# Down projections of two FFNs as seven half products per pair of blocks, with more low parts summed by transfer

## The chip, the cores and the metric

The kernel runs on one core of a Trainium2 chip. The metric is the time of one execution on the device in microseconds. A profile is one execution taken by the hardware profiler; its times are microseconds unless marked ns. Engines are named as in the profile: PE (TensorE matmul), PEld (its weight loads), ACT (ScalarE), DVE (VectorE), POOL (GpSimd), SP (SyncE). POOL and SP issue the DMA transfers here; the accumulating ones go through POOL, plain loads mostly through SP.

## The reference

One encoder layer over 512 tokens with a model width of 1024, in float32. What concerns this change are the two FFNs; between them stands a mixer of a Fourier part and an attention part.

```python
def rms_norm(x, g):
    xf = x.astype(jnp.float32)
    y = xf * lax.rsqrt(jnp.mean(xf * xf, axis=-1, keepdims=True) + EPS)
    return (y * g.astype(jnp.float32)).astype(x.dtype)

def swiglu(h, w_gate, w_up, w_down):
    return (jax.nn.silu(h @ w_gate) * (h @ w_up)) @ w_down

x = x + 0.5 * swiglu(rms_norm(x, ffn1_norm), ffn1_w_gate, ffn1_w_up, ffn1_w_down)
...
x = x + 0.5 * swiglu(rms_norm(x, ffn2_norm), ffn2_w_gate, ffn2_w_up, ffn2_w_down)
return rms_norm(x, final_norm)
```

The hidden width D_FF is 2752, that is 21 columns of 128 and a tail of 64.

## The kernel before

**Numbers in two parts.** Matmuls run on the type float32r, which keeps fewer bits. So each operand is split: a high part is the value rounded by a cast on ScalarE (`nc.scalar.copy`, shown as CAST), and a low part is what is left, value minus high part. A product is three matmuls: high x high, high x low, low x high. The low part is made in one of two ways. `lows` (L130 for all callers) is one subtraction on VectorE. `rest_by_dma` (L159, L160) has ScalarE write the negated high part and POOL issue an accumulating transfer that adds the value to it from memory; what needs the low part then waits for the landing.

**Layout.** The tokens lie along the free dimension (S = 512) and the model width in eight blocks of 128 (KD = 8): `x[0]` to `x[7]`. All weights in two parts live in `ring`, twelve slots of 1024 elements (NS = 12), which `take` and `give` hand out first in, first out: a slot that comes free is written next by whoever takes it, so a cast into it waits for the last matmul that reads what was there.

**One FFN** (`ffn`) goes through the 21 columns in groups (`GROUPS1`, `GROUPS2`). The first group is computed plainly (`gate`, `evacuate`). From then on `seven` computes a column's gate and up products by the Strassen-Winograd scheme: seven products a11, a12, s1, s2, s4, s3, a22 of half the width in place of eight (`multiply`, lines L432, L436, L441). s1 to s4 are sums of weights that VectorE forms (`combine`, L406) in the temporaries `s12` and `s34`, of which there is one buffer each. `prepare` makes a column's weights while the column before is multiplied. The only low part that goes by transfer there is that of a22 (`single`, L400, 256 KB). The product a22 of a column stands behind a12 of the next one; that of the last column is called `rest` and stands inside the group's down projection. `seven` runs one column ahead of its group, so its last column belongs to the next group.

**Down projection.** For each of the eight blocks d, `down` loads the group's weights (`raw_dn`), makes the high part on ScalarE (L172) and the low part on VectorE (L130), and multiplies with the group's activations `at`, three 512-wide matmuls for each column (L186, out `dn`). `residual` (L575) then adds half of the sum to `x[d]`. With six columns in a group the columns 3 to 20 of the first FFN take three groups; the second FFN has groups of 6, 6 and 7.

**Order.** On PE and SP the order is that of the code. On ACT, DVE and POOL a scheduler has fixed the order when the kernel was built; at run time each engine works strictly in that order, so an instruction that waits holds up all behind it on its engine.

Of the kernel before, what the change touches and what calls it, by code (L numbers as in the profile page):

```python
# [88 lines left out]
def encoder(ctx, tc, A, out):  # L89
# [19 lines left out]
    def bank(name):  # L109
        return pp.tile([P, S], F32, tag="bank", name=name)  # L110
# [173 lines left out]
    def ffn(norm, after, wgu, wd, wdt, groups, opening, closing):  # L284
# [6 lines left out]
        with tc.tile_pool(name=f"act{n_}", bufs=1) as ap, tc.tile_pool(name=f"sums{n_}", bufs=2) as sp:  # L291
            room(ap, 128)
            acts = ap.tile([P, PLACES * 2 * S + ROOM], F32R, name=f"at{n_}")
            at = acts[:, FRONT + LOWER : FRONT + LOWER + PLACES * 2 * S].rearrange("p (n a b) -> p n a b", a=2, b=S)
            rt = ap.tile([P, 7 * KH * S + -(-PART_AT[-1] // ROOM) * ROOM], F32R, name=f"rt{n_}")
            wt, raws = [], {}
# [76 lines left out]
            def give(*ts):  # L373
                for t in ts:
                    taken[:] = [q for q in taken if q is not t]
                    (shared if any(t is q for q in slots[KD:]) else own).append(t)

            def prepare(j):

# [9 lines left out]
                def both(names, src):  # L389
                    hi, lo = (take() for _ in range(2))  # L390
                    nc.scalar.copy(hi, src)  # L391
# [27 lines left out]
            def seven(js, done):  # L419
# [37 lines left out]
                def step(j, w, n):  # L457
# [33 lines left out]
                    elif n == 9:  # L491
                        multiply(b["r"], "a22", "t4", w, False)
                        u, i = b["u"], place(j)
                        h, l = at[:, i, 0], at[:, i, 1]
                        kept(u[:, HALF:], b["r"], "a22" in WIDE)
                        nc.vector.tensor_tensor(out=u, in0=b["g"], in1=u, op=ALU.mult)
                        nc.scalar.copy(h, u)
                        lows(l, u, h)
                        del banks[j]
# [16 lines left out]
            def down(d, group, gi):  # L516
# [23 lines left out]

                return steps

            def token_weights(d, group):
# [36 lines left out]
            for gi, group in enumerate(groups):  # L580
# [4 lines left out]
                else:  # L585
# [19 lines left out]
                    def rest():  # L605
                        evacuate(at[:, place(n_plain - 1)], n_, pss[n_plain - 1], norm)

                def added(d, ps):
# [3 lines left out]
                    if ahead:  # L612
                        f, *a = ahead.pop(0)
                        f(*a)

                waiting, downs = [], []
                for d in range(KD):
# [35 lines left out]

    def evacuate(at, n_, pss, norm):
        g = tp.tile([P, S], F32, tag="g", name=f"g{n_}p")
        u = tp.tile([P, S], F32, tag="u", name=f"u{n_}p")
        h, l = at[:, 0], at[:, 1]
        if len(pss) == 2:
            nc.vector.tensor_tensor(out=g, in0=pss[0], in1=norm.rb, op=ALU.mult)
            nc.vector.tensor_tensor(out=u, in0=pss[1], in1=norm.rb, op=ALU.mult)  # L660
            nc.scalar.activation(g, g, AF.Silu)
            nc.vector.tensor_tensor(out=u, in0=g, in1=u, op=ALU.mult)
            nc.scalar.copy(h, u)
# [904 lines left out]
```

## Time and profile before

| | |
|---|---|
| times of three runs | 818.92, 818.92, 819.8 us (median 818.92) |
| the profiled execution's own time | 818.9 us |
| its span, first to last instruction | 817.1 us |
| mean granted clock | 0.998 |
| matmuls of the FFN columns (L432, L436, L441) | 2520 |
| matmuls of the down projections of whole blocks (L186, out `dn`) | 945 |
| accumulating transfers from POOL (L160) | 53 |

How to read the profile: a group of instructions is named by line, engine, operation and tiles (out<-in); "busy" is the time in which at least one of them ran, "mean ns" the length of one, "idle before" the time in which the engine stood still just before them and what ended it. A row of the timeline gives the start, the length, the engine, the line and how many instructions followed each other without a gap. Matmuls are pipelined, so the distance between starts says more than the length of one.

### The profile page before, as it was taken

What the parts mean: (1) busy time and instruction counts of PE and PEld (TensorE: products, weight loads), DVE (VectorE), ACT (ScalarE), POOL (GpSimd) and SP (SyncE); (2) the same over time, 40 slices, a digit from 0 to 9 for tenths busy, and PEclk for the clock granted to TensorE, in tenths of its full rate; (3) what the DMA queues carried; (4) which work ended last, traced back from release to release, by engine and by line L of the source; (5) the groups of instructions that cost most, each with busy time, mean ns of one, the idle gap of its engine ahead of it and who ended that gap; (6) DMA issues with size and microseconds to landing.
All of it is one profiled execution on the core that took longest, in us unless ns stands there. A gap on an engine that the chain in (4) does not pass through costs nothing.

```text
span 817.1 us, 13011 instructions
## 1 busy us (share of the span) xinstructions
PE 810.0 (99%) x4936; PEld 729.1 (89%) x4936; DVE 652.0 (80%) x1080; ACT 503.5 (62%) x871; POOL 67.7 (8%) x75
## 2 busy tenths in 40 slices
PE   9999999999999999999999999999999999999997
PEld 7888998899989998889998888899988998899987
DVE  7997997489856867799998588999955997489674
ACT  7883774167623735689999449557733674267462
POOL 0320000000000000221000003100100000000001
PEclk9999999999999999999999999999999999999999
DMA  7874553345343423342101236564443553345223
GB/s 258 198 176 167 150 130 91 123 130 168 85 138 94 130 71 117 130 149 65 66 26 52 79 101 145 128 188 143 134 116 111 153 144 79 134 130 145 60 78 103
DMA packets 37534, 99.75 MB, mean 122 GB/s; under 512 B 4448, under 2 KB 10720, under 8 KB 37472
## 3 DMA queue, kind: packets, MB, share of 16 engines
q1 hardware_dynamic: 27776, 82.61, 31.4%
q0 software_dynamic: 8832, 15.34, 11.0%
q10 hardware_dynamic: 864, 0.98, 0.3%
q8 instruction: 38, 0.62, 0.3%
q14 instruction: 24, 0.20, 0.1%
HBM read 93.41 MB, written 2.10 MB: 117 GB/s over the span
## 4 chain that ended last, share of the span: by engine, by line
PE 96%; DMA 1%; DVE 1%; ACT 1%; issue 0%; POOL 0%; POOLq 0%; DVEq 0%; ACTq 0%
PE dn L186 24%; PE r L436 12%; PE mix L186 8%; PE r L441 8%; PE gu L186 8%; PE q L436 4%; PE q L441 4%; PE r L432 4%; PE p L432 4%; PE q L432 4%; PE gu L740 3%; PE p L441 2%; PE mix L1234 2%; PE mix L1200 2%; PE mix L1038 1%; PE mix L1039 1%
## 5 line engine op out<-in xcount | busy, mean ns | idle before, releaser
L186 PE MATMUL dn<-at,ring 128*128 128x512 f32 x900 | 202.8, 380 | 0.8 <-DVE ring L130 0.8
L186 PEld LDWEIGHTS dn<-at,ring 128*128 128x128 f32 x900 | 167.9, 188 | 29.8 <-DVE ring L130 1.2
L441 PE MATMUL r<-rt,ring 128*128 128x256 f32 x560 | 154.3, 276 | 0.0
L436 PE MATMUL r<-rt,ring 128*128 128x256 f32 x840 | 147.1, 276 | 0.0
L436 PEld LDWEIGHTS r<-rt,ring 128*128 128x128 f32 x840 | 127.1, 188 | 1.6
L441 PEld LDWEIGHTS r<-rt,ring 128*128 128x128 f32 x560 | 105.1, 188 | 0.2
L391 ACT CAST ring<-s 128x1024 fp32r<-128x1024 f32 x70 | 73.6, 1051 | 35.6 <-PE r L436 16.5
L130 DVE TENSOR_TENSOR ring<-s,ring 128x1024 fp32r<-128x1024 f32 x70 | 85.2, 1217 | 12.1 <-ACT ring L391 10.1
L575 DVE SCALAR_TENSOR_TENSOR gx<-dn,gx 128x512 f32<-128x512 f32 x61 | 41.8, 688 | 61.9 <-PE dn L186 61.8
L172 ACT CAST ring<-raw_dn 128x768 fp32r<-128x768 f32 (+3 forms) x58 | 45.3, 783 | 70.6 <-PE dn L186 55.8
L441 PE MATMUL q<-rt,ring 128*128 128x256 f32 x280 | 77.0, 275 | 0.0
L160 POOL DMA_DIRECT2D ring<-in_wgu x38 | 32.9, 866 | 470.9 <-ACT u L450 372.8
L130 DVE TENSOR_TENSOR ring<-raw_dn,ring 128x768 fp32r<-128x768 f32 (+3 forms) x58 | 51.5, 891 | 9.0 <-ACT ring L172 4.9
L441 PEld LDWEIGHTS q<-rt,ring 128*128 128x128 f32 x280 | 52.6, 188 | 0.0
L130 DVE TENSOR_TENSOR ring<-raw_g,ring 128x1024 fp32r<-128x1024 f32 x35 | 42.7, 1219 | 9.8 <-PE p L432 9.5
L436 PE MATMUL q<-rt,ring 128*128 128x256 f32 x280 | 49.8, 277 | 0.0
L186 PE MATMUL gu<-ring 128*128 128x512 f32 x216 | 48.9, 381 | 0.0
L432 PE MATMUL r<-rt,ring 128*128 128x512 f32 x140 | 48.5, 383 | 0.0
L432 PE MATMUL q<-rt,ring 128*128 128x512 f32 x140 | 48.4, 382 | 0.0
L432 PE MATMUL p<-rt,ring 128*128 128x512 f32 x140 | 48.3, 382 | 0.0
L186 PEld LDWEIGHTS gu<-ring 128*128 128x128 f32 x216 | 40.4, 188 | 6.9
L391 ACT CAST ring<-raw_g 128x1024 fp32r<-128x1024 f32 x35 | 36.8, 1051 | 13.6 <-DMA raw_g<-in_wgu 10.6
(277 smaller groups left out, 1658.6 us busy)
## 6 DMA issues: line engine op xcount, KB each, us to landing
raw_g<-in_wgu SPq DMA_DIRECT2D x35, 512.0 KB, 3.8
raw_u<-in_wgu SPq DMA_DIRECT2D x35, 512.0 KB, 4.5
raw_dn<-in_wd SPq DMA_DIRECT2D x40, 384.0 KB, 3.2
ring<-in_wgu POOLq DMA_DIRECT2D x35, 256.0 KB, 4.3
raw_gu<-in_wgu SPq DMA_DIRECT2D x12, 512.0 KB, 3.9
raw_o<-in_wo SPq DMA_DIRECT2D x8, 512.0 KB, 3.3
raw_dn<-in_wd SPq DMA_DIRECT2D x8, 448.0 KB, 3.3
raw_wq<-in_wins SPq DMA_DIRECT2D x4, 512.0 KB, 3.4
```

The lines of the kernel that those rows point to most:

```text
L130: nc.vector.tensor_tensor(out=lo, in0=src, in1=asf(hi), op=ALU.subtract)
L160: nc.gpsimd.dma_start(out=lo, in_=src, accum_op=ALU.add)
L172: nc.scalar.copy(hi[:, :n, :], raw[:, :n, :])
L186: nc.tensor.matmul(ps, a, b, start=first and b is mhi and a is whi, stop=last and a is wlo)
L391: nc.scalar.copy(hi, src)
L432: nc.tensor.matmul(turned(ps), whi[:, ks], turned(m), start=start, stop=False, skip_group_check=True)
L436: nc.tensor.matmul(ps[:, t], whi[:, ks], m[:, o * HALF :][:, t], start=start and o == 0, stop=False, skip_group_check=True,)
L441: nc.tensor.matmul(o, wlo[:, ks], m, start=False, stop=stop, skip_group_check=True)
L575: nc.vector.scalar_tensor_tensor(out=x[d][:, t], in0=ps[:, t], scalar=0.5, in1=x[d][:, t], op0=ALU.mult, op1=ALU.add)
L740: nc.tensor.matmul(turned(pss[c]), w[:, k % 2, c], turned(m[k]), start=k == 0 and m is hh and w is hi, stop=k == KD - 1 and w is lo,)
L1200: nc.tensor.transpose(pts[n][:, c * P : (c + 1) * P], prob[t, b, c][:, kc * P : (kc + 1) * P], ident)
L1234: nc.tensor.matmul(turned(outs[t, b]), w, turned(p), start=kc == 0 and i == 0, stop=kc == 3 and i == 1)
```

## The change

The 24 columns 3 to 14 of the first FFN and 2 to 13 of the second now form six groups of four (`GROUPS1`, `GROUPS2`); the first and the last group of each FFN keep their way. In these six *fast* groups the down projection is done by the same scheme as the columns: the eight blocks are paired as *rows*, i and i + 4 for i = 0 to 3, the four columns as two pairs and the tokens as two halves. A row is seven products P1 to P7 of two column pairs each (c = 0, 1), each with 256 tokens in three matmuls: 42 matmuls 256 wide, where the plain way takes 24 that are 512 wide for the same two blocks and four columns. Three banks r, q and p serve a row; P6, P7 and P4 add onto P1 in r, P3 onto P5 in q, and VectorE adds half of what stands in the bank to `x` after each product (L656 in the new file).

New functions: `quarter_operands` makes the two parts of the activations and of their four sums from a pair of columns (`tq`); `quarter_weights` loads a row's weights, has VectorE form four sums (`sq`, in the same two temporaries `s12` and `s34`, by even and odd row) and makes all three low parts by transfer (`rest_by_dma`): 256 KB for a11 and a12, 512 KB for the sums, 128 KB for a22, in four slots of the ring. `fast_down` runs the products in the order of `TURNS`, in which P7 and P4 of a row stand among the products of the next, and asks for row i + 2 after P2 of row i + 1; the next group's first column is prepared between the rows. `keep` takes the place of the two-part copy at a column's end. Also new: the low part of a column's gate weights (512 KB) goes by transfer in the fast groups and in the group behind each, and the room for the descriptors of POOL's transfers is set to 8192 bytes.

```diff
-GROUPS1 = ((0, "t", 1, 2), range(3, 9), range(9, 15), range(15, 21))
-GROUPS2 = ((0, "t", 1), range(2, 8), range(8, 14), range(14, 21))
+GROUPS1 = ((0, "t", 1, 2), range(3, 7), range(7, 11), range(11, 15), range(15, 21))
+GROUPS2 = ((0, "t", 1), range(2, 6), range(6, 10), range(10, 14), range(14, 21))
+TURNS = "P1 P5 P2 P6 P3", "P1 P7 P5 P2 P4 P6 P3", "P7 rest P4"
...
+            def split(i0, i1, c, src, transfer=False):
+                h, l = (quarters[:, i0:i1, c, o] for o in range(2))
+                nc.scalar.copy(h, src)
+                if transfer:
+                    rest_by_dma(l, h, src)
+                else:
+                    lows(l, src, h)
...
+            def quarter_operands(c, u1, u2):
+                b11, b12, b21, b22 = (u[:, o * HALF : (o + 1) * HALF] for u in (u1, u2) for o in range(2))
+                t = sp.tile([P, 4, HALF], F32, tag="turned", bufs=1, name=f"tq{n_}_{len(where)}_{c}")
+                for o, (p, q) in enumerate(((b12, b11), (b22, t[:, 0]), (b22, b12), (b21, t[:, 1]))):
+                    nc.vector.tensor_tensor(out=t[:, o], in0=p, in1=q, op=ALU.subtract)
+                split(0, 1, c, u1[:, :HALF].unsqueeze(1))
+                split(1, 3, c, u2.rearrange("p (o b) -> p o b", o=2))
+                split(3, 7, c, t, c == 0)
...
-                    lows(lo, src, hi)
+                    if src is g and by_dma(j):
+                        rest_by_dma(lo.rearrange("p (a b) -> p a b", b=P), hi.rearrange("p (a b) -> p a b", b=P), wgu[2 * j])
+                    else:
+                        lows(lo, src, hi)
...
+            def quarter_weights(i, group, gi):
+                n, j0 = len(group), group[0]
+                raw = wp.tile([P, KD, P], F32, tag="raw", name=f"raw_q{n_}_{i}_{gi}")
+                for h in range(2):
+                    nc.sync.dma_start(out=raw[:, h * n : (h + 1) * n], in_=wd[i + 4 * h][:, j0 : j0 + n, :])
...
+                s_ = sp.tile([P, 2 * S], F32, tag=("s12", "s34")[i % 2], bufs=1, name=f"sq{n_}_{i}_{gi}")
...
+                first, hi, lo, rest_ = (take() for _ in range(4))
...
+                nc.scalar.copy(ah, raw[:, :n])
+                rest_by_dma(al, ah, wd[i][:, j0 : j0 + n, :])
+                nc.scalar.copy(hi, s_)
+                rest_by_dma(lo, hi, s_)
+                nc.scalar.copy(bh, a22)
+                rest_by_dma(bl, bh, wd[i + 4][:, j0 + 1 : j0 + n : 2, :])
...
+                return w, {"P2": (first,), "P7": (hi, lo), "P4": (rest_,)}
...
+                    for c in range(2):
+                        hi, lo = w[a][c]
+                        for v, m in ((hi, 0), (hi, 1), (lo, 0)):
+                            nc.tensor.matmul(
+                                out, v, quarters[:, o, c, m], start=opens and c == 0 and v is hi and m == 0,
...
+                    give(*ws[i][1].get(name, ()))
+                    nc.vector.scalar_tensor_tensor(
+                        out=x[i + d][:, t], in0=out, scalar=0.5, in1=x[i + d][:, t], op0=ALU.mult, op1=ALU.add
+                    )
...
+                    multiply(i, p)
+                    if p == "P2" and i + 1 < n and i:
+                        ws[i + 1] = quarter_weights(i + 1, group, gi)
+                    if (i, p) == (1, "P7"):
+                        nxt = prepare(groups[gi + 1][0] + 1)
...
-    nc = bacc.Bacc("TRN2", target_bir_lowering=False, num_devices=1)
+    nc = bacc.Bacc("TRN2", target_bir_lowering=False, num_devices=1, dynamic_dma_scratch_size=8192)
```

Three places show how the order has moved. The names: `ring` are the weights' slots, `r0_7` the bank of column 7 of FFN 0, `u` and `g` its up and gate halves, `raw_dn0_2_1` the down weights of block 2 in group 1, `sq0_1_1` the sums of row 1 in group 1, `raw_q` a row's weights, `tq` the sums of the activations. The last number is the buffer's.

First ScalarE, before, in the first FFN where group 1's down projection begins:

```order
L391 CAST ring_61<-s34_0_10_1445 128x1024
L497 CAST at0_128<-u0_8_1280 128x512
L489 COPY u0_9_1377<-r0_9_1285 128x256
L479 ACTIVATE g0_9_1309<-g0_9_1309 128x512
L172 CAST ring_61<-raw_dn0_2_1_1450 128x768
L450 COPY u0_9_1377<-r0_9_1285 128x256
L497 CAST at0_128<-u0_9_1377 128x512
L172 CAST ring_61<-raw_dn0_3_1_1475 128x768
```

And now, at the same place, where group 1 ends with the columns 6 and 7:

```order
L505 COPY p10_7_1068<-r0_7_1067 128x256
L616 CAST ring_61<-sq0_0_1_1174 128x1024
L618 CAST ring_61<-raw_q0_0_1_1171 128x256
L161 ACTIVATE ring_61<-ring_61 128x1024
L161 ACTIVATE ring_61<-ring_61 128x256
L505 COPY u0_6_1062<-r0_6_960 128x256
...
L616 CAST ring_61<-sq0_1_1_1191 128x1024
L544 COPY u0_7_1168<-r0_7_1067 128x256
L618 CAST ring_61<-raw_q0_3_1_1352 128x256
L534 ACTIVATE g0_7_1091<-g0_7_1091 128x512
L161 ACTIVATE ring_61<-ring_61 128x1024
```

Before, a block's weights took ScalarE one cast; now the sums of a row take a cast and a negation of 1024 elements each, and between the two for row 1 stand a copy of column 7's s3, a cast for row 3 and the silu of column 7.

On VectorE, before, at the start of group 1's down projection:

```order
L130 TENSOR_TENSOR at0_128<-u0_8_1280,at0_128 128x512
L490 TENSOR_TENSOR u0_9_1377<-u0_9_1377,p50_9_1326 128x256
L575 SCALAR_TENSOR_TENSOR gx_69<-dn0_0_1_1380,gx_69 128x512
L130 TENSOR_TENSOR ring_61<-raw_dn0_2_1_1450,ring_61 128x768
L452 TENSOR_TENSOR u0_9_1377<-r0_9_1285,u0_9_1377 128x256
L496 TENSOR_TENSOR u0_9_1377<-g0_9_1309,u0_9_1377 128x512
```

And now:

```order
L132 TENSOR_TENSOR at0_128<-u0_6_1062,at0_128 128x2x256
L608 TENSOR_TENSOR sq0_2_1_1277<-raw_q0_2_1_1274 128x256 x2
L502 TENSOR_TENSOR g0_7_1091<-q0_7_1116,g0_7_1091 128x256
L132 TENSOR_TENSOR at0_128<-tq0_4_1_1105,at0_128 128x4x256
L608 TENSOR_TENSOR sq0_2_1_1277<-sq0_2_1_1277,raw_q0_2_1_1274 128x256
L656 SCALAR_TENSOR_TENSOR gx_69<-rd0_1_0_1205,gx_69 128x256
```

The first sums of row 2 (`sq0_2_1`) now stand ahead of the low parts of the turned activations (`tq0_4_1`) that the second product reads; they are written to the buffer that row 0's sums had, which a transfer of POOL reads.

On POOL, where nothing but one 256 KB transfer per column stood in the first FFN's groups before, the stretch that belongs to group 1's down projection is now:

```order
L162 DMA ring_61<-sq0_0_1_1174 128x1024
L162 DMA ring_61<-in_wd1 128x2x128
L162 DMA ring_61<-in_wd1 128x512
L162 DMA ring_61<-sq0_1_1_1191 128x1024
L162 DMA ring_61<-in_wd1 128x2x128
L162 DMA ring_61<-in_wd1 128x512
L162 DMA ring_61<-sq0_2_1_1277 128x1024
L162 DMA ring_61<-in_wd1 128x2x128
L162 DMA ring_61<-in_wgu1 128x1024
L162 DMA ring_61<-in_wd1 128x512
L162 DMA ring_61<-sq0_3_1_1355 128x1024
```

The next column's gate weights (`in_wgu1`, 512 KB) stand ahead of row 3's first part (`in_wd1 128x512`) and its sums.

More of the change, by code (lines that the diff above doesn't have):

```diff
@@ L376, in give, with fast, by_dma, keep @@
                     (shared if any(t is q for q in slots[KD:]) else own).append(t)
+            group_of = {j: (gi, i) for gi, group in enumerate(groups) for i, j in enumerate(group) if gi}
+            def fast(gi):
+                return 0 < gi < len(groups) - 1
+            def by_dma(j):
+                return fast(group_of[j][0]) or fast(group_of[j][0] - 1)
+            halves_of, late = {}, []
+            def split(i0, i1, c, src, transfer=False):
[5 more added lines that the diff above has]
+                    lows(l, src, h)
+            def keep(j, u):
+                gi, i = group_of[j]
+                if fast(gi):
+                    halves_of[j] = u
+                    if i % 2:
+                        quarter_operands(i // 2, halves_of.pop(j - 1), halves_of.pop(j))
+                    return
+                p = place(j)
+                h, l = at[:, p, 0], at[:, p, 1]
+                def put():
+                    nc.scalar.copy(h, u)
+                    lows(l, u, h)
+                late.append(put)
+                if not (fast(gi - 1) and i == 0):
+                    late.pop()()
+            def quarter_operands(c, u1, u2):
[6 more added lines that the diff above has]
+                split(3, 7, c, t, c == 0)
             def prepare(j):
@@ L605, in rest @@
                     def rest():
-                        evacuate(at[:, place(n_plain - 1)], n_, pss[n_plain - 1], norm)
+                        if fast(1):
+                            evacuate(None, n_, pss[n_plain - 1], norm, lambda u: keep(n_plain - 1, u))
+                        else:
+                            evacuate(at[:, place(n_plain - 1)], n_, pss[n_plain - 1], norm)
                 def added(d, ps):
@@ L614, in added @@
                         f(*a)
+                if fast(gi):
+                    ready = fast_down(group, gi, rest)
+                    continue
                 waiting, downs = [], []
@@ L652, in ffn, with evacuate @@
                 free.extend(where[j] for j in group)
-    def evacuate(at, n_, pss, norm):
+    def evacuate(at, n_, pss, norm, keep=None):
         g = tp.tile([P, S], F32, tag="g", name=f"g{n_}p")
         u = tp.tile([P, S], F32, tag="u", name=f"u{n_}p")
-        h, l = at[:, 0], at[:, 1]
+        h, l = (at[:, o] if at is not None else None for o in range(2))
         if len(pss) == 2:
```

70 lines of the change are left out of this document (66 added, 4 removed).

## The prediction

> **What bounds the kernel now.** First the page: how busy each engine is, and what the chain of work that ended last is made of.
>
> ```profile
> span 817.1 us, 13011 instructions
> PE 810.0 (99%) x4936; PEld 729.1 (89%) x4936; DVE 652.0 (80%) x1080; ACT 503.5 (62%) x871; POOL 67.7 (8%) x75
> ...
> PE 96%; DMA 1%; DVE 1%; ACT 1%; issue 0%; POOL 0%; POOLq 0%; DVEq 0%; ACTq 0%
> ```
>
> TensorE is the bound, and it hardly ever waits. So fewer matmul columns are worth their full time, and any new wait of TensorE costs its full length. Next, TensorE's timeline in the first FFN: start, length, and how many matmuls follow each other.
>
> ```profile
> 134.49 20.42 PE L186 MATMUL dn<-at,ring 128*128 128x512 f32 x92
> 155.72 7.75 PE L186 MATMUL dn<-at,ring 128*128 128x512 f32 x34 [0.81 <-DVE ring L130]
> ...
> 163.31 0.39 PE L436 MATMUL r<-rt,ring 128*128 128x256 f32 x2
> ...
> 164.33 0.39 PE L436 MATMUL r<-rt,ring 128*128 128x256 f32 x2
> ```
>
> A 512-wide matmul takes a place of 0.220 us: 92 of them in 20.42, less the tail of the last (0.16). Between 163.31 and 164.33 stand nine 256-wide ones: 0.1133 us each. The 0.81 is the longest wait in the FFNs.
>
> Last come the rates of the helpers, from the timelines of ScalarE and VectorE inside a column's products. What counts is the distance from one start to the next, since their instructions overlap a little.
>
> ```profile
> 98.22 0.64 ACT L159 ACTIVATE ring<-ring 128x512 fp32r<-128x512 f32 x1 [0.53 <-PE r L436]
> 98.76 0.35 ACT L450 COPY u<-r 128x256 f32<-128x256 f32 x1
> 99.01 1.05 ACT L391 CAST ring<-s 128x1024 fp32r<-128x1024 f32 x1
> 99.96 0.62 ACT L497 CAST at<-u 128x512 fp32r<-128x512 f32 x1
> ...
> 97.30 1.21 DVE L130 TENSOR_TENSOR ring<-s,ring 128x1024 fp32r<-128x1024 f32 x1
> 98.43 0.68 DVE L496 TENSOR_TENSOR u<-g,u 128x512 f32<-128x512 f32 x1
> 99.03 0.68 DVE L406 TENSOR_TENSOR s<-raw_u 128x512 f32<-128x512 f32 x1
> 99.67 0.42 DVE L445 TENSOR_TENSOR g<-q,u 128x256 f32<-128x256 f32 x1
> 100.02 0.68 DVE L406 TENSOR_TENSOR s<-s,raw_g 128x512 f32<-128x512 f32 x1
> ```
>
> ScalarE: 0.95 for 1024 elements, 0.54 for 512, 0.25 for a 256 copy (I take 0.31 for a 256 cast, a little more than the copy). VectorE: 1.13, 0.60 and 0.35.
>
> **The change on TensorE.** The order has 576 fewer 512-wide matmuls of the down projections and 1008 more 256-wide ones. So 576 x 0.220 = 126.8 us go and 1008 x 0.1133 = 114.2 come: a gain of 12.6 us, 2.1 in each of the six fast groups. This is all that the change can win.
>
> **VectorE and ScalarE as sums** are not in the way. A fast group has 4 x 9.44 us of column products (12 x 0.220 + 60 x 0.1133 each) and 4 rows of 42 x 0.1133 = 4.76: 56.8 us on TensorE. By the distances above VectorE has about 50 us in it (7.3 a column, 5.7 for the operands, 3.9 a row: four sums and seven additions of 256), ScalarE about 46. In full durations VectorE would have 57.8; that is a bound too, but a mild one. More POOL issues (188 instructions after 75) cost nothing by themselves: 21 a group at 0.86 are 18 us.
>
> ```profile
> L160 POOL DMA_DIRECT2D ring<-in_wgu x38 | 32.9, 866 | 470.9 <-ACT u L450 372.8 <-DVE u L496 43.0 <-DVE s L406 23.1
> ```
>
> The gate's low parts that become transfers are asked for a column (9.44 us) ahead and have that column's products to land in, as the one transfer per column has now; if they did not, a group would lose the 1.13 us of VectorE that each takes now. The smaller descriptor space I take at nothing: no row shows a wait for it; POOL now waits for ScalarE alone in 373 us.
>
> **The transfers in order** are where I expect the loss. A low part "by transfer" is a chain: the ring slot comes free, ScalarE casts, ScalarE negates, POOL issues, the transfer adds, and only then may the third matmul of the product start. These are the answers on DMA: one 512 KB accumulating transfer each, one of 128 KB, then a stretch with accumulating transfers alone and one with plain loads alone.
>
> ```profile
> at<-in_wgu POOLq DMA_DIRECT2D x1, 512.0 KB, 5.5
> ring<-in_wgu POOLq DMA_DIRECT2D x1, 512.0 KB, 7.6
> ring<-in_wgu POOLq DMA_DIRECT2D x1, 512.0 KB, 5.3
> ring<-in_wgu POOLq DMA_DIRECT2D x1, 512.0 KB, 5.2
> rt<-b POOLq DMA_DIRECT2D x1, 128.0 KB, 2.7
> DMA packets 757, 0.76 MB, mean 191 GB/s; under 512 B 62, under 2 KB 744, under 8 KB 756
> DMA packets 1312, 3.30 MB, mean 412 GB/s; under 512 B 401, under 2 KB 401, under 8 KB 1312
> ```
>
> So 512 KB takes 5.3 us from issue to landing; behind another one it adds its own data time, 2.75 us at 191 GB/s (256 KB: 1.4). A quicker end: 2.7 us for 128 KB and 2.06 for the other 384 KB are 4.8. A slower end: 7.6, met beside other transfers. I take 5.3, the middle of three rows that agree.
>
> Now the first fast group by hand. T is the end of s3 of its last column, when the seven half products begin; each product is 6 x 0.1133 = 0.68, and its low weight is wanted 0.23 after its start.
>
> *Row 0.* The sums' slot is the one that a12 of the last column frees, at T-6.7. Cast 0.95, a 256 cast 0.31, negation 0.95: the transfer is issued at T-4.4 and lands at T+0.9. The sums of row 2 use the same temporary, so VectorE's first sum of row 2 stands until then, and the low parts of the turned operands (1024 wide) stand behind it: three of 0.35, then 1.13, done at T+3.1. Second product P5 needs them at T+1.1. **Stall 1: 2.0.**
>
> *Row 1.* Its sums' slots are those of s3, the last product of the column, so the cast starts at T+0.1 at best. Cast, a copy, a cast, the silu (which waits for VectorE behind the same transfer, T+1.9), negation: issued at T+3.5, landed at T+8.8. P5 of row 1 needs it at T+5.0, with stall 1 at T+7.0. **Stall 2: 1.8.**
>
> *Row 2.* Slots free when P7 of row 0 ends, T+6.8; cast and negation to 8.8, landed 14.1; P5 of row 2 wants it at 9.8 + 3.8 = 13.6. **Stall 3: 0.5.**
>
> *Row 3, first part.* Its slot frees with P7 of row 1 at T+13.3, together with that of the next column's gate weights, which stand ahead on ScalarE (0.95) and on POOL (512 KB). Issue of the gate's transfer 14.4, landed 19.7, row 3's 256 KB 1.4 later: 21.1; P1 of row 3 wants it at 13.2 + 4.3 = 17.5. **Stall 4: 3.6.**
>
> *Row 3, sums.* 2.75 behind: 23.9, wanted at 14.5 + 7.9 = 22.4. **Stall 5: 1.5.**
>
> Together 9.4 us a group, where a column's own products hid such a transfer before: the single one per column had 9.4 us to land in. Six groups: 56.4 lost, 12.6 won. With 4.8 in place of 5.3 the same steps give 8.0 a group, with 7.6 they give 16.3; TensorE then ends 35 or 85 us later.
>
> [...]
>
> **The sum.** The profiled execution took 818.9 us, its span plus 1.8, and is the median of the three runs (818.92 to 819.8). 818.9 - 12.6 + 56.4 = 862.7; I say 862. A difference under 0.2% (1.6 us) can't be told from none.
>
> **Rivals.**
>
> *Faster: the transfers are hidden.* The stalls cancel the gain at 2.1 us a group. If every transfer landed as the quickest row does, in 2.7, stall 1 shrinks to the 0.75 of VectorE's own row, stall 2 to 0.2, stall 4 to 0.7: 1.65 a group, and 818.9 + 6 x (1.65 - 2.1) = 816; with no stall 806. For it: that row. Against it: four rows of 5.2 and more for the size in question. 0.17, of which 0.04 lies within 0.2% of now.
>
> *Between: transfers as quick as plain loads.* The 2.7 of the 128 KB row and the other 384 KB at the plain loads' 412 GB/s make 3.65 us, and 1.3 for 512 KB behind another. The same steps then give 0.75, 1.1, 0, 1.7 and 0.4: 4.0 a group, 818.9 - 12.6 + 24 = 830. No row shows it for 512 KB, and 191 GB/s speaks against it. 0.08. [...]
>
> *The 16 DMA engines fill up.* Around the down stage of a group (from T-4.4, some 34 us with the stalls) stand 4.06 MB of accumulating transfers and 3.1 MB of loads: 21.3 + 7.5 = 29 us at the two rates above. If the critical transfers share with loads, the 7.6 row holds: 904. 0.09.
>
> *The clock falls.* Here are windows of before's end, whose last matmuls end at 811.73; the column after POOL is the granted clock.
>
> ```profile
> 810.99 0.74 PE L1395 MATMUL xt<-ident,gx 128*128 128x128 f32 x5
> ...
> 811.70:814.40 2.70, 0.03 (x1) 0.00 (x0) 1.60 (x4) 0.80 (x2) 0.55 (x1) 1.00 0.95 352
> 814.42:817.10 2.68, 0.00 (x0) 0.00 (x0) 0.00 (x0) 0.00 (x0) 0.00 (x0) 0.50 0.38 127
> ...
> 0.78 4.00 PE L685 MATMUL busy<-const-bfloat16-1.0 128*128 128x512 bf16 x9 [0.78 <-PEq L1551]
> 4.91 2.28 PE L740 MATMUL gu<-ring 128*128 128x512 f32 x8
> ```
>
> 2.7 us after the last matmul the clock is granted at half. Stall 4 is longer than that. At the start nine matmuls take 4.00 us, 0.42 each, twice the later place; such a stretch of about 4.7 us costs 2.35. Once per group this is 14 us more: 877. 0.08. [...]
>
> *My forecast:* 0.58, 854 to 875.
>
> So faster 0.13, same 0.04, slower 0.83. The range reaches from 828, just under the between case, to 900, nearly the slow end of the transfers; it leaves out the faster and same cases (0.17) and little else.
>
> **What would show it.** In the profile after: 256-wide matmuls of the half products at places of 0.113 (right), idle time of TensorE of some 9 us in each fast group, released by accumulating transfers of the sums and by VectorE's 1024-wide low parts at the second product; stalls at P5 of rows 0, 1 and 3 and at P1 of row 3; accumulating 512 KB transfers of 5 us or more. Wrong: TensorE's idle time in a group under 2.1 us, transfers of 3 us, or VectorE busy without a break in the groups while TensorE waits (then its sums, not the transfers, are the bound).

## The result, and the profile after

Before 819.36 us (median of 4 runs, 818.92 to 821.16), after 993.06 (4 runs, 991.33 to 1002.81): ratio 1.214, 95% interval 1.206 to 1.222. The forecast was slower, 862, with a range up to 900; the kernel lost 174 us and not 43. The profiled execution took 991.33.

The page of the changed kernel, the same rows as before:

```profile
span 989.6 us, 14683 instructions
PE 864.4 (87%) x5368; PEld 782.1 (79%) x5368; DVE 694.3 (70%) x1299; ACT 616.4 (62%) x1036; POOL 177.8 (18%) x188
...
PE 31%; issue 31%; DMA 25%; ACT 5%; POOL 3%; DVE 3%; POOLq 0%; DVEq 0%; SPq 0%; ACTq 0%
```

No engine is full any more, and a quarter of the chain that ended last is transfers ("issue" is time in which the engine waited for nothing that the profile shows). TensorE's waits by what ended them (us in total, times, longest):

```profile
PE qd L649 <- DMA ring<-sq: 42.7, 20, 4.3
PE r L496 <- DMA ring<-in_wgu: 34.2, 18, 4.3
PE q L487 <- ACT p L505: 13.3, 6, 2.2
PE qd L649 <- DVE at L132: 10.6, 6, 1.8
PE r L487 <- ACT u L544: 8.7, 7, 1.7
PE rd L649 <- DMA ring<-in_wd: 5.1, 3, 3.2
PE rd L649 <- DVE gx L656: 2.2, 7, 0.6
```

The rows `qd` and `rd` (L649) are the half products, 61 us; the rows `r` and `q` (L496, L487) are the columns' products, 56 us, where the kernel before had no wait at all.

Next, busy time by stretch (engines in order PE, PEld, DVE, ACT, POOL; then the granted clock, the DMA share, GB/s). Before: the first group's columns and its down projection.

```profile
73.70:129.20 55.50, 55.50 (x426) 53.21 (x425) 50.42 (x81) 37.77 (x67) 5.17 (x6) 1.00 0.47 129
129.20:163.30 34.10, 33.29 (x154) 28.14 (x153) 17.63 (x26) 9.41 (x13) 0.00 (x0) 1.00 0.40 116
```

After: columns and half products of the first two fast groups.

```profile
74.10:119.40 45.30, 39.38 (x282) 36.71 (x281) 29.88 (x57) 30.84 (x54) 11.59 (x12) 0.96 0.74 164
119.40:157.40 38.00, 27.51 (x179) 25.88 (x177) 22.34 (x48) 17.20 (x24) 8.65 (x9) 0.87 0.79 164
157.40:207.10 49.70, 40.98 (x283) 38.05 (x282) 31.62 (x62) 31.67 (x56) 11.54 (x12) 0.93 0.69 151
207.10:245.10 38.00, 28.13 (x178) 26.74 (x177) 22.40 (x48) 16.91 (x24) 8.68 (x9) 0.82 0.77 163
```

Each stretch after has idle time of TensorE, and in each the clock falls below 1.00, to 0.82 in one: that is a third loss, beside the two kinds of wait.

To put all three on one scale I took, for every matmul of the FFNs' columns and down projections, the distance from its start to the next start, less its place at full clock (0.220 for 512, 0.1133 for 256). What is left is lost time; it is called a wait where TensorE stood still for over 0.06 us before the next, half clock where the granted clock was 0.5.

| us lost | columns | down stages | sum |
|---|---|---|---|
| waits | 63.2 | 68.3 | 131.5 |
| matmuls at half clock | 15.8 | 24.2 | 40.0 |
| the rest (edges of both, places a little longer) | 9.3 | 6.6 | 15.9 |

That is 187.3 us, 2.7 in the kernel before; 184.6 less the 12.6 won by fewer matmul columns are 172.0, and the span grew by 172.5. The experiments are measured on this scale too.

### The profile page after: what moved, and what is told of

Same layout as the page of the kernel before. It is cut to its first block, busy times and chain, and to the rows that moved or that the text cites. A ratio compares the mean times of both kernels' runs of the same rounds, so it can differ in the third digit from the quotient of the medians.

```text
span 989.6 us, 14683 instructions
## 1 busy us (share of the span) xinstructions
PE 864.4 (87%) x5368; PEld 782.1 (79%) x5368; DVE 694.3 (70%) x1299; ACT 616.4 (62%) x1036; POOL 177.8 (18%) x188
## 4 chain that ended last, share of the span: by engine, by line
PE 31%; issue 31%; DMA 25%; ACT 5%; POOL 3%; DVE 3%; POOLq 0%; DVEq 0%; SPq 0%; ACTq 0%
DMA ring<-in_wgu 11%; DMA ring<-sq 8%; PE dn L188 6%; DMA raw_q<-in_wd 4%; PE r L496 3%; PE mix L188 3%; PE r L491 2%; PE gu L895 2%; POOL ring L162 2%; PE r L487 2%; PE p L487 2%; PE gu L188 2%; PE q L491 2%; ACT ring L161 2%; PE qd L649 1%
## 5 line engine op out<-in xcount | busy, mean ns | idle before, releaser
L496 PE MATMUL r<-rt,ring 128*128 128x256 f32 x560 | 160.8, 287 | 34.2 <-DMA ring<-in_wgu 34.2
L496 PEld LDWEIGHTS r<-rt,ring 128*128 128x128 f32 x560 | 109.1, 195 | 38.1 <-DMA ring<-in_wgu 37.9
L161 ACT ACTIVATE ring<-ring 128x1024 fp32r<-128x1024 f32 (+2 forms) x145 | 110.9, 778 | 31.1 <-PE p L487 16.3
L649 PE MATMUL qd<-at,ring 128*128 128x256 f32 x288 | 54.6, 315 | 54.0 <-DMA ring<-sq 42.7
L649 PE MATMUL rd<-at,ring 128*128 128x256 f32 x576 | 91.1, 311 | 7.3 <-DMA ring<-in_wd 5.1
L649 PEld LDWEIGHTS rd<-at,ring 128*128 128x128 f32 x576 | 84.4, 221 | 10.2 <-DMA ring<-in_wd 5.7
L649 PEld LDWEIGHTS qd<-at,ring 128*128 128x128 f32 x288 | 44.1, 213 | 59.8 <-DMA ring<-sq 47.2
L496 PE MATMUL q<-rt,ring 128*128 128x256 f32 x280 | 78.2, 279 | 0.0
L188 PE MATMUL dn<-at,ring 128*128 128x512 f32 x324 | 74.8, 380 | 0.4 <-DVE ring L132 0.4
L188 PEld LDWEIGHTS dn<-at,ring 128*128 128x128 f32 x324 | 60.5, 188 | 11.1 <-DVE ring L132 0.8
L162 POOL DMA_DIRECT2D ring<-in_wd x48 | 56.7, 1206 | 54.6 <-DVE sq L608 27.1
L487 PE MATMUL q<-rt,ring 128*128 128x512 f32 x140 | 52.3, 408 | 13.9 <-ACT p L505 13.3
L656 DVE SCALAR_TENSOR_TENSOR gx<-rd,gx 128x256 f32<-128x256 f32 x96 | 40.4, 423 | 33.1 <-PE rd L649 32.8
L487 PE MATMUL r<-rt,ring 128*128 128x512 f32 x140 | 50.5, 396 | 8.7 <-ACT u L544 8.7
L487 PE MATMUL p<-rt,ring 128*128 128x512 f32 x140 | 54.3, 419 | 0.0
L496 PEld LDWEIGHTS q<-rt,ring 128*128 128x128 f32 x280 | 53.6, 191 | 0.0
```

The lines of the kernel that those rows point to most:

```text
L161: nc.scalar.activation(lo, asf(hi), AF.Copy, scale=-1.0)
L162: nc.gpsimd.dma_start(out=lo, in_=src, accum_op=ALU.add)
L188: nc.tensor.matmul(ps, a, b, start=first and b is mhi and a is whi, stop=last and a is wlo)
L487: nc.tensor.matmul(turned(ps), whi[:, ks], turned(m), start=start, stop=False, skip_group_check=True)
L496: nc.tensor.matmul(o, wlo[:, ks], m, start=False, stop=stop, skip_group_check=True)
L649: nc.tensor.matmul(out, v, quarters[:, o, c, m], start=opens and c == 0 and v is hi and m == 0, stop=c == 1 and v is lo, skip_group_check= ...
```

## The experiments

All 14 against the kernel before on the same chip (its medians 818.9 to 819.6); the edits are to the changed kernel.

**1. Gate low parts by VectorE.**

```diff
             def by_dma(j):
-                return fast(group_of[j][0]) or fast(group_of[j][0] - 1)
+                return False
```

> The low part of every column's gate weights is made by one VectorE subtraction again, as in the kernel before; all else is as changed. In the changed kernel's trace TensorE loses, against its places of 0.220 and 0.113 us, 63 us in waits among the columns' products (37 of them at L496 for the gate's transfers), 68 in waits of the down stages and 40 in matmuls that run at the half clock behind waits. Theory (each wait costs its length, and the half clock follows the waits): the 37 go and their share of the half clock, 40 x 37/131 = 11, with them: 993 - 48 = 945 us, and the waits for ring<-sq in the down stages stay at about 46. Rival 1 (VectorE has no room: 35 more subtractions of 1.13 us are 40 us): the waits only change their name, to VectorE, and the time stays above 975. Rival 2 (the transfers crowd each other: 35 fewer of 512 KB make the others land sooner): the down stages' waits fall too, below 930.

919.5 us (1.122, 1.118 to 1.127), 74 less. Its waits of over 5 us:

```profile
PE qd L649 <- DMA ring<-sq: 43.9, 20, 4.3
PE q L487 <- ACT p L505: 11.1, 12, 1.2
PE qd L649 <- DVE at L132: 10.6, 6, 1.8
```

The waits for the gate are gone and no new one came in their place. The columns' loss fell from 88.2 to 16.0, their half clock to nothing; the down stages kept theirs (95.9 after 99.0). It is more than the theory's 48, since the waits for ScalarE (u, L544) and all of the columns' half clock went too. Both rivals fall: the time is under the 930 of the second, but the down stages, which it said would gain, kept their loss.

**2. Low parts of the rows' sums by VectorE** (`rest_by_dma(lo, hi, s_)` becomes `lows(lo, s_, hi)`).

> The low parts of the four sums of a row's weights (512 KB, 24 of them) are made by one VectorE subtraction of 1024 elements in place of a negation and a transfer; all else as changed. Theory: the chain to the second product of a row gets shorter by a negation (0.95) and a transfer (5.3) and longer by 1.13, some 5 us, more than the waits it caused (2.1 each); so the 46 us of waits for ring<-sq go, the 11.6 at the first P5 for VectorE behind the same temporary too, and their share of the half clock, 40 x 58/131 = 18: 993 - 76 = 917 us, while the columns' waits for the gate's transfers stay at about 37. Rival (VectorE is the bound once it has 4.5 us more in a group of 57): waits for VectorE take their place, 960 or more.

962.6 us (1.176, 1.169 to 1.183): 30 us less, where 76 were expected. Its waits of over 5 us:

```profile
PE r L496 <- DMA ring<-in_wgu: 38.4, 19, 4.2
PE rd L649 <- DMA ring<-in_wd: 27.7, 6, 5.0
PE q L487 <- ACT p L505: 13.3, 6, 2.2
PE qd L649 <- DVE gx L656: 9.2, 6, 2.3
PE r L487 <- ACT u L544: 6.7, 7, 1.5
```

The waits for `sq` and for VectorE at the first P5 went, as the theory had it, but a wait stepped out from behind them: P1 of row 3 in every group, 4.6 us each, for the row's own 256 KB.

**3. The grouping alone** (`fast` returns False).

> Groups of four columns as changed, but every group goes the old way: whole blocks in the down projections, no half products, gate low parts by VectorE. Theory: the grouping alone costs next to nothing, 819 to 824 us, with TensorE busy 99%. Rival (a down stage of 21 us in place of 32 is too short to prepare the next column's weights, and six more group ends cost 2 us or more each): 831 or more.

819.6 us (1.0004, 0.9994 to 1.0013). Groups of four cost nothing; the theory holds.

**4. One fast group** (`fast` returns `gi == 1 and not n_`).

> Only the columns 3 to 6 of the first FFN form a fast group; the other groups of four go the old way (gate low parts by transfer only in that group and the one behind it). Theory: the cost is one of each group by itself, (993 - 819)/6 = 29 us, a little less for the first: 843 to 850 us. Rival (the groups make it worse for each other, since a fast group ends with late weights for the next one's columns): one alone costs under 18, 837 or less.

854.7 us (1.043, 1.039 to 1.046): 35 for one, a little above the theory; six of them cost 174, so the groups don't make it worse for each other.

**5. Gate and sums by VectorE** (1 and 2 together).

> Both edits of the first two experiments: gate low parts and the low parts of the rows' sums by VectorE; only a row's own weights (256 and 128 KB) and the first pair's turned operands still go by transfer. The first run, 919.5, has left in its down stages 47 us of waits for ring<-sq, 11.6 for VectorE behind the sums' temporary and 25 in matmuls at half clock. Theory (costs add, and the second run's 28.7 us of waits for a row's own 256 KB came from the gate's 512 KB ahead of it on POOL): 919.5 - 59 - 20 + 8 for VectorE's own lateness (13.7 in place of 5.7) = 849, waits for in_wd under 5. Rival 1 (a row's 256 KB is late by itself): its 28 us stay, 875 or more. Rival 2 (VectorE, with 9 us more in each group than before, is the bound): TensorE waits for VectorE in the columns too, 870 or more.

898.1 us (1.096, 1.093 to 1.098). The part on the 256 KB held in the main: 28.7 lost for `in_wd` in the second run are 9.6 here (under 5 was expected), so most of it was the gate's transfer ahead of it on POOL. But the sum missed by 49. The timeline of ScalarE and TensorE at the first group's second product (start, length, engine, line, idle before):

```profile
118.10 0.40 ACT L618 CAST ring<-raw_q 128x256 fp32r<-128x256 f32 x1 [4.02 <-DMA raw_q<-in_wd]
...
120.05 1.04 ACT L394 CAST at<-tq 128x1024 fp32r<-128x1024 f32 x1
...
121.15 0.58 PE L649 MATMUL qd<-at,ring 128*128 128x256 f32 x1 [5.73 <-ACT at L394]
```

ScalarE waits 4.02 us for weights of row 3, for a cast that its order has put ahead of those of row 1 (the "cast for row 3" in the order shown with the change). The operand that TensorE needs next stands behind it. TensorE loses 35 us at this place over six groups; how much of that is the cast's doing, the ninth run tells.

**6. No transfers but a22 of the columns** (5, and `lows` for a11/a12, a22 and the turned operands).

> As the run beside it, and the low parts of a row's own weights and of the first pair's turned operands by VectorE too: in the fast groups only a22 of each column still goes by transfer, as in the kernel before. Theory (transfers are the trouble, but VectorE cannot carry everything): VectorE's sum in a group becomes 50 + 9 + 4 x 0.95 + 1.1 = 64 us where TensorE has 57, so about 7 us a group are lost to VectorE, 806 + 42 = 848, all waits for VectorE or for ScalarE behind it. Rival (VectorE keeps up, its sum being too high): 830 or less.

874.9 us (1.067, 1.065 to 1.069), above both forecasts: the columns lose 1.5 us in all, the down stages 67, of which 19 for ScalarE's cast of `tq`, 14 for VectorE's low part of `tq`, 12 for its updates of x and 14 at half clock.

**7. Waits filled with work** (on 1).

```diff
                     out = ps[i, b][:, :HALF]
+                    if name == "P5" and i != 1:
+                        for _ in range(10):
+                            nc.tensor.matmul(ps[i, b], *one, start=True, stop=True)
```

> The first experiment (gate low parts by VectorE), with ten 512-wide bf16 matmuls of constants put ahead of the second product P5 of the rows 0, 2 and 3, into the bank that P5 then starts anew: 2.2 us of work at the full clock in waits that are 2.3 us long on average. Nothing of the result changes. Theory (the half clock follows TensorE's standing still): the stretches at half clock in the down stages fall from 65 us to under 25, the 25 us that the matmuls lose in them to under 10, and the time from 919.5 to about 903 though 180 matmuls are added. Rival (the half clock comes from something else, such as the dense 256-wide stream, or the clock's windows don't count such work): the half clock stays and the time is 919 or more.

913.7 us (1.115, 1.113 to 1.118). The granted clock of the first run, and of this one:

```profile
core 0: 914.0 us, clock 0.967
```

```profile
core 0: 911.7 us, clock 0.995
```

The stretches at half clock in the FFNs fell from 58 us to 6.8, the matmuls' loss in them from 24.7 to 3.1: the half clock follows TensorE's standing still, and the rival falls. Of the 40 us of added matmuls about 22 fell into waits, so the gain is small: 6 us between the medians, whose runs overlap (915.85 to 922.75 and 912.59 to 916.71), and 2.3 between the two profiled executions, where 16 were expected.

**8. Sums wanted later** (5, and `TURNS = "P1 P2 P5 P6 P3", "P1 P2 P7 P4 P5 P6 P3", "P7 rest P4"`).

> As the run with gate and sums by VectorE, and TURNS changed to P1 P2 P5 P6 P3 for row 0 and P1 P2 P7 P4 P5 P6 P3 after it: the first product of a row that needs sums comes 0.68 (row 0) or 1.36 us later, and a row's weights are asked for earlier, row 3's ahead of the next column's gate. Theory (what is left in the down stages is lateness of the chain to P5): those waits shrink by about 1 us each, 24 of them, with some half clock: 20 to 30 us under that run, about 825. Rival (VectorE's sum over the group is the limit, not the order): within 5 us of that run.

892.7 us (1.089, 1.087 to 1.091), 5 less. The wait for the cast of `tq` fell from 35 to 1 us, but the one for VectorE's low part of it rose from 8 to 14, that for ScalarE's p in the columns from 7 to 13, and 11 for VectorE's updates of x at P5 are new. Nearer to the rival.

**9. The late cast tied back** (on 5).

```diff
-                nc.scalar.copy(bh, a22)
+                tc.keep_in_program_order(nc.scalar.copy(bh, a22))
```

> The fifth run (gate and sums by VectorE, 898.1) with one thing more: ScalarE's cast of a row's a22 (L618) is tied behind what stands ahead of it in the code on ScalarE. In that run row 3's cast stood ahead of the casts of row 1's sums and of the turned operands tq and waited 4.0 us for its own load, though its product comes some 17 us later; TensorE then lost 35 us at P5 of row 0 for the cast of tq (L394) and 14.7 in matmuls at half clock. Theory (that one cast holds up ScalarE): the 35 fall to under 10, the half clock by half, 898 - 26 - 7 = 865 us, and ScalarE's 30 us of waits for raw_q under 12. Rival (the operands of the last pair are late by themselves, whatever stands ahead): within 8 us of 898.

875.6 us (1.069, 1.067 to 1.070), 22.5 less. Its waits:

```profile
PE qd L649 <- DVE at L132: 12.4, 6, 2.1
PE qd L649 <- ACT at L394: 9.0, 6, 1.5
PE rd L649 <- DMA ring<-in_wd: 8.9, 6, 2.6
PE rd L649 <- DVE gx L656: 7.3, 17, 0.7
```

One cast in the wrong place cost 22 us. What is left at P5 of row 0 is the operand's own lateness: its column ends shortly before the half products begin. The half clock stayed (15.0).

**10. The same tie in the changed kernel alone.**

> The changed kernel itself (993) with that cast tied back and nothing else. Its ScalarE waited 33 us for raw_q in 12 places. Theory (a part of the 46 us of waits for ring<-sq and of the columns' 25 for ScalarE is that cast, the larger part the transfers): 960 to 980 us. Rival (the transfers alone set those waits): within 10 us of 993.

979.8 us (1.198, 1.194 to 1.202), the upper end of the theory. Lost for `sq` 33 (46 before), for ScalarE in the columns 10 (26), for VectorE behind the temporary 0 (12); but row 3's own weights now 28 (6), the gate 44 (37). The tie is worth 22 us in the ninth run and 13 here, where the transfers stand behind it.

**11. Experiment 6 with the tie and the order of 8.**

> The sixth run (no transfers but a22 of the columns, 874.9) with the cast tied back and the order P1 P2 P5 P6 P3 and P1 P2 P7 P4 P5 P6 P3 of the eighth. The sixth has 18.9 us of waits for the cast of tq (L394), 14.2 for its low part (L132), 11.8 for VectorE's updates of x (L656), 14 in matmuls at half clock. Theory (order on ScalarE, then lateness of the chain to P5): the 18.9 go, the 14.2 fall to 8, half of the half clock goes: 875 - 19 - 6 - 7 = 843. Rival (VectorE's 64 us in a group of 57 are the limit): 865 or more, waits for VectorE in their place.

893.4 us (1.091, 1.089 to 1.093): 18 worse. The rival's time and place came: waits for VectorE are 57 of the 68 us lost in waits. Its reason, the sum of VectorE's work, isn't shown by that: the fourteenth run has the same work and is 18.7 us faster.

**12. Row sums formed by GpSimd** (on 11; `nc.gpsimd.tensor_tensor` for the four sums).

> As the run beside it, and the four sums of a row's weights are formed by GpSimd, which has nothing else to do there, in place of VectorE: 16 instructions of 0.35 us a group leave VectorE, 5.6 us, and GpSimd takes about 0.74 us for each (its 256-wide product before the end of the kernel). Theory (VectorE is what TensorE waits for by now): 8 to 15 us under that run. Rival (GpSimd's sums are late, 2.9 us a row, or the two engines slow each other down): equal to that run or slower, with longer VectorE instructions while GpSimd works.

902.0 us (1.102, 1.100 to 1.103), 9 worse. VectorE's low part of a row's own weights in the run before, then here, beside GpSimd's sums (count, busy, mean ns):

```profile
L132 DVE TENSOR_TENSOR ring<-raw_q,ring 128x512 fp32r<-128x512 f32 x24 | 16.6, 690 | 1.3 <-PE rd L649 1.3
```

```profile
L132 DVE TENSOR_TENSOR ring<-raw_q,ring 128x512 fp32r<-128x512 f32 x24 | 25.6, 1066 | 2.6 <-PE rd L649 1.9 <-ACT ring L616 0.7
...
L608 POOL TENSOR_TENSOR sq<-raw_q 128x256 f32<-128x256 f32 x48 | 41.7, 929 | 48.9 <-DVE ring L132 48.9
```

690 ns became 1066, and it goes with the overlap: the 18 of the 24 that overlap one of GpSimd's sums took 889 to 1252 ns, the 6 that don't 692 or 693. The two slow each other down, as the rival said: GpSimd's sums took 929 to 1049 ns on average, where a product of this width took 735 in the kernel before.

**13. Plain groups of four, gate by transfer** (3, with `by_dma` True).

> Groups of four columns, all down projections the old way (the third run, 819.6), but the gate's low parts of every column by transfer as in the changed kernel: 38 accumulating transfers of 512 KB with nothing of the half products beside them. Theory (as the prediction had it, such a transfer is asked for early enough by itself, and it was the crowd of ScalarE's work and transfers of the fast groups that made it late): 820 to 826 us, waits for ring<-in_wgu under 4. Rival (the chain of cast, negation and transfer is longer than the time that the order gives it, crowd or none): the 37 us of waits and their half clock come back, 850 or more.

869.8 us (1.062, 1.057 to 1.066), where without the transfers it is 819.6. The rival holds: the transfers cost 50 us without the work of the half products beside them. One such transfer in the timeline: the last matmul of a12 of the running column, the negation, the issue, the wait.

```profile
141.81 0.28 PE L496 MATMUL p<-rt,ring 128*128 128x256 f32 x1
...
142.07 1.06 ACT L161 ACTIVATE ring<-ring 128x1024 fp32r<-128x1024 f32 x1 [0.91 <-PE p L487]
...
143.42 0.86 POOL L162 DMA_DIRECT2D ring<-in_wgu  x1 [28.45 <-ACT ring L161]
...
148.80 0.39 PE L496 MATMUL r<-rt,ring 128*128 128x256 f32 x1 [0.64 <-DMA ring<-in_wgu]
```

The negation writes into the slot that a12 has just read. From 142.07 to 148.80 are 6.7 us, of which 5.4 are the transfer, and the next column wants the low part 6.1 us after that a12. Of the 33 gate transfers that have a running column before them, 20 have their negation start so, as a12 ends, and 13 from 0.3 to 2.7 us after it. TensorE waits for 21 of them, 21.4 us in all, in two kinds: 16 waits of 0.2 to 0.8 us (8.3 in sum) are behind transfers of 5.2 to 5.5 us, which the chain alone makes late, and 5 waits of 1.8 to 3.4 us (13.1 in sum) behind transfers that took 7.0 to 8.3.

**14. Experiment 6 with the tie alone.**

> The sixth run (no transfers but a22 of the columns, 874.9) with ScalarE's cast of a row's a22 tied back and the order of the half products as changed: the eleventh run (893.4) without its other order. Theory (the tied cast helps here as it did in the ninth run, and the later sums of the eleventh were what cost, since they hand VectorE two updates at once): 853 to 862 us. Rival (with all low parts on VectorE its order is full, and tying the cast moves the wait to VectorE only): 870 to 893.

874.7 us (1.068, 1.066 to 1.070): no gain over the sixth run, which is the rival's case; 15.1, 16.5 and 16.9 us are lost for the cast and the low part of `tq` and for x. So the 18.7 us of the eleventh are the other order's. By which step it costs that much here, when the same order gained 5 in the eighth, stays open. No version beat the kernel before: what is won is 2.1 us a group, and the best of those with six fast groups still lose about 11 there.

## Why the prediction was wrong

The direction was right and its mechanism was there, the down stages' waits; two further losses of the same order had been priced at nothing, or left to a rival with a chance of 0.08.

**TensorE's gain: right.** 5368 matmuls, half products at places of 0.114 (median), and the account above closes with 12.6.

**VectorE and ScalarE as sums: right, and not enough.** 54.0 and 48.6 us of busy time in the second fast group, neither full. But ScalarE's order was read for what stands in it and not for what each thing there waits for: the cast for row 3 was named, and its load, 4 us late, wasn't priced. The ninth run shows 22 us for it where the other waits don't cover it.

**The gate's low parts: the step that failed.** "The gate's low parts that become transfers are asked for a column (9.44 us) ahead and have that column's products to land in" - and so they were put at nothing. The order asks for them that early, but the slot of the low part comes free only with a12 of the running column, as the thirteenth run's rows show: 6.1 us are there for 1.06 of negation and 5.4 of transfer. That is 50 us in plain groups (13 less 3) and 74 in the changed kernel (1). A transfer of 5.4 us misses by under 1 us there; most of the waiting is for transfers that take longer, as the next paragraph shows. The single a22 of a column lands no sooner (256 KB, median 5.9 us in the changed kernel), but its product stands later, behind a12 of the column after. The price named in case it failed, 1.13 us a group, was that of VectorE and not of the wait.

**The transfers' time: right in the middle, too short where it counted.** 5.3 was taken, and the sums' 24 transfers have a median of 5.5, but they are of two kinds: 13 took 4.5 to 5.6 us and 11 took 6.1 to 8.2. Two of the second fast group, that of row 2 with the plain load issued beside it, then that of row 3 (KB, us to landing):

```profile
ring<-sq POOLq DMA_DIRECT2D x1, 512.0 KB, 7.0
raw_u<-in_wgu SPq DMA_DIRECT2D x1, 512.0 KB, 4.4
...
ring<-sq POOLq DMA_DIRECT2D x1, 512.0 KB, 4.5
```

The long ones are those of row 0 in all six groups and of row 2 in five, and beside each a 512 KB load of the next column's weights (`raw_u`) is issued, at most 1.2 us away; row 2's in the sixth group, with that load 1.0 us behind it, took 5.6, and those of rows 1 and 3, without it, 4.5 to 5.4. For the gate it is alike: 12 of its 18 waits, 29.9 of their 34.2 us, stand behind transfers of 6.8 to 8.0. Had each of these transfers taken 5.3 us, the waits for the gate would be about 11 us and those for the sums about 26 in place of 42.7; this is an estimate that shortens each wait by its transfer's excess and leaves out what moves behind it. So the 7.6 row, which the prediction set aside as the slow end, was the better figure for transfers that meet others. What makes them long is read from such rows; no run took the loads away.

**The down stages: right in sum, wrong in place**, so that the sum is in part luck. Mean waits per group, by product:

| us | P5 row 0 | P5 row 1 | P5 row 2 | P1 row 3 | P5 row 3 | other | sum |
|---|---|---|---|---|---|---|---|
| predicted | 2.0 | 1.8 | 0.5 | 3.6 | 1.5 | 0 | 9.4 |
| measured | 3.15 | 0.54 | 3.42 | 0.85 | 1.78 | 0.47 | 10.2 |

In the first group TensorE's timeline shows how they shift:

```profile
122.05 0.50 PE L649 MATMUL qd<-at,ring 128*128 128x256 f32 x2 [1.59 <-DMA ring<-sq]
124.31 0.50 PE L649 MATMUL qd<-at,ring 128*128 128x256 f32 x2 [1.76 <-DVE at L132]
...
126.46 1.48 PE L649 MATMUL qd<-at,ring 128*128 128x256 f32 x6
127.74 2.11 PE L649 MATMUL rd<-at,ring 128*128 128x256 f32 x12
...
139.05 1.12 PE L649 MATMUL qd<-at,ring 128*128 128x256 f32 x4 [3.68 <-DMA ring<-sq]
```

P5 of row 0 waits twice, first for its own sums, whose transfer took 6.7 us, then for VectorE behind the temporary, as described. After it the clock is at half (six matmuls in 1.28 us, 0.213 each), and that slowness gives row 1's transfer the time it lacked: its wait became a slower stretch. Row 2, which was to profit from row 1's wait, takes it over, and its own transfer is one of the long ones (6.8). In the sixth group no stretch at half clock falls on the rows 0 to 2 and row 2's transfer takes 5.6; there the rows wait much as predicted, 1.73 for row 1, 0.97 for row 2 and 3.21 for P1 of row 3:

```profile
850.23 0.73 PE L649 MATMUL qd<-at,ring 128*128 128x256 f32 x4 [1.73 <-DMA ring<-sq]
...
856.24 0.74 PE L649 MATMUL qd<-at,ring 128*128 128x256 f32 x4 [0.97 <-DMA ring<-sq]
...
863.25 2.08 PE L649 MATMUL rd<-at,ring 128*128 128x256 f32 x8 [3.21 <-DMA ring<-in_wd]
```

That P1 of row 3 would wait behind the gate's transfer is shown by the second run, where nothing else holds it up: 4.6 us, and by the fifth, where it falls to 1.4 with the gate's transfer gone.

**The clock: a rival that should have been part of the sum.** It had 0.08 and 14 us, one trip a group, after a wait of over 2.7. It came 23 times in the FFNs and cost 40 us; the seventh run shows that it follows the standing still (58 us of half clock, 6.8 with the waits filled). The error was in the bound: 2.7 us was one reading, at the kernel's end, and not the least standing still that brings it about.

Together, of the 131 us above the forecast: 72 are the columns' loss that went with the gate's transfers (first run), 24 the down stages' half clock, 15 what the columns still lose in that run, mostly for ScalarE, and 18 what else the down stages lose, waits that are 12 longer on this scale than computed and places a little longer. That makes 129, which is what the profiled execution lies above the forecast; the median lies 1.7 higher. The rival with full DMA engines had the long transfers right (its 7.6), whatever makes them long, and put them at 41 us more in the down stages; there the idle time came to 61.2 us where 56.4 were computed, and most of what came on top lies in the columns. The smaller descriptor space lost nothing in the third run (819.6 us), which has it too but few transfers; with many, no run has the old one.

## What to carry to other kernels

A transfer in place of an engine's instruction is asked for when its buffer comes free and not when the code asks (here 6.1 us ahead of its use and not 9.44): find the last reader of that buffer, and count from there to the first use. Take the time of a transfer from rows that have the same transfers beside them, and not from a median: the ones waited for can be the long ones (11 of the sums' 24 took 6.1 to 8.2 us here, with a median of 5.5 over all). Where an engine that never waited begins to, price each wait together with the slow clock behind it (here 40 us beside 131.5 of waits), and look for the wait that the one removed has covered. In an order that a scheduler has fixed, an early place for something that isn't needed yet is a cost as soon as its input is late (22.5 us for one cast, in the ninth run).

## What the runs showed of the hardware

- **The half clock goes by a fixed grid.** In six traces (after, 1, 4, 6, 7, 13) every stretch at half clock before the kernel's end begins on a grid of 3.413 us and lasts one or two of its cells; in the changed kernel 23 such stretches begin at 105.05 us, 125.53, 139.18 and so on up to 886.70, 229 cells after the first, 19 of them 3.413 us long and 4 of them 6.827. Each of these 50 has ahead of it a cell in which TensorE stood still for 1.76 us or more in all; the longest standing still in a cell that brought none is 1.92 (in the changed kernel 1.86). So 1.8 to 1.9 us of standing still within one cell, a little over half of it, brought the half clock in some cells and not in others, and over 1.92 us brought it in all.
- **VectorE and GpSimd hinder each other.** With each working element by element on two SBUF inputs (twelfth run), VectorE's 512-wide low parts of a row's weights went from 690 ns to 1066 on average (692 where they overlapped none of GpSimd's, 889 to 1252 where they did), and GpSimd's 256-wide sums took 929 to 1049 ns on average, 735 for a product of this width in the kernel before.
